# An encoder trunk in float32 on one core: ten by-k tiles, bias parts between pairs, and a wide form in layer 1

## The chip, the cores and the metric

The kernel runs on one core of a Trainium2 chip. The metric is the device time of one execution in microseconds (us); the profile is one execution taken by the hardware profiler. The core's engines are TensorE (PE in the profile; PEld is its weight load), VectorE (DVE), ScalarE (ACT), GpSimd (POOL) and SyncE (SP), which here issues all transfers from device memory.

## The reference

Two layers over 256 tokens of width 2048, all in float32. A conditioning vector gives six vectors of 2048 a layer, which shift, scale and gate.

```python
cond = jax.nn.silu(c)
for l in range(DEPTH):
    mod = cond @ w_ada[l] + b_ada[l]                 # 2048 x 12288
    sh_a, sc_a, g_a, sh_m, sc_m, g_m = split(mod, 6)
    h = _rmsnorm(x) * (1.0 + sc_a) + sh_a
    proj = h @ w_in[l]                               # dq, dk, dv, cq, ckv, kr
    ...                                              # two kinds of attention; one has a relative-position bias
    x = x + g_a * (concat(out_a, out_b) @ w_o[l])
    h = _rmsnorm(x) * (1.0 + sc_m) + sh_m
    x = x + g_m * (square(relu(h @ w_mlp_in[l])) @ w_mlp_out[l])
return _rmsnorm(x, final_norm_g)
```

## The kernel before

Activations lie as features by tokens: 16 slices (k) of 128 features by 256 tokens. A weight matrix is cut into tiles of 128 columns; a tile's product with all 16 slices is 16 products of 128x128 weights with 128x256 activations.

**Three forms of a product.** Float32 values are split into two fp32r parts, `hi` (ScalarE, L143, L575, L593) and `lo` (VectorE, L144, L581, L594). The *narrow* form (`mac`, L175 to 181) multiplies in three matmuls of 256 columns: hi by hi, hi by lo, lo by hi. The *wide* form (`wide`, L190 to 201) has hi and lo of the activations side by side: one matmul of 512 columns (L199) and one of 256 (L200), into a bank of its own whose two halves are added afterwards (`joined`, L864, or in the update itself). The *whole* form (L243) multiplies unsplit float32; the profile counts two matmuls for each of its products.

**By k.** After a norm the slices of h come one pair at a time, so the first product is done by k (`by_k`): for pair p (slices 2p, 2p+1) all open column tiles are multiplied and summed up in open PSUM banks (8 in all, tag `b`). Before the change this is 12 tiles in 6 banks, two to a bank, in both layers and for both norms: in layer 0's first norm in the whole form for pairs 0 to 5 (`WHOLE`) and narrow for pairs 6 and 7, elsewhere narrow. The remaining columns follow tile by tile; in the MLP in the wide form.

**The head.** `setup` broadcasts c, loads and transposes x, and prepares the position bias. The modulation vectors are sums on VectorE (L306): each 1 MB block of `w_ada` gives one slice of one vector, 192 blocks in all, loaded into the 5 `raw` buffers. `first_norm_then_by_k` (L630) needs for pair p four blocks: two for the shift (g 0), two for the scale (g 1); L316 finishes the scale. Then L573 makes the modulated pair `hf` on ScalarE. In the order of the program, pair p issues its weights (L224, in the `hi` and `lo` buffers, four of each), makes the marks of a bias part (L452, L456, L458), makes pair p+1 ready (L563, four blocks, L573, L575), multiplies (L243), and then has the work that `FILL` names for p: a bias part (L468, L469, 16 matmuls into bank `pb`, out by four copies L472), the lambdas or the rope tables. `EARLY` says after which pair the first three quarters of a second product (`w_d`, four tiles, `later`, two banks) are done in the whole form.

**Rates.** Later blocks of `w_ada` are loaded by credit: every call of `weights` adds `rate`, and each full credit issues one block, summed at the next call.

**Order.** Program order is the priority; the builder's scheduler may let a ready instruction pass one that it believes is waiting. `behind` adds an order by hand. Each engine then runs its queue in order; SyncE's queue too, so a transfer that waits for a buffer holds up all behind it.

Of the kernel before, what the change touches and what calls it, by code (L numbers as in the profile page):

```python
# [94 lines left out]
EARLY = {4: (0, 1), 6: (2,)}  # L95
# [3 lines left out]
RATE_A0, RATE_A1, RATE_A2, RATE_K, RATE_M = 1.1, 0.5, 0.7, 0.6, 0.66  # L99
FILL = "0|1|2|l3|r"  # L100


class Trunk:
# [142 lines left out]

    def tokens_by_k(self, pss, w, xs, first, last):
# [86 lines left out]
    def setup(self):  # L334
# [18 lines left out]
        for h in range(2):  # L353
            for t in range(2):
                xt[t][h] = self.wp.tile([P, D // 2], F32, tag=("hi", "lo")[h], name=self.name("xt"), bufs=4)
                nc.sync.dma_start(xt[t][h], io["x"][t, :, D // 2 * h : D // 2 * h + D // 2])
        self.bias_setup()
        self.rel = [self.bias_rel(0)]
        for j in range(4):
# [3 lines left out]
            nc.scalar.activation(self.cond[:, c], ps, AF.Silu)  # L363
        self.x = cp.tile([P, NK, T], F32, name="x")
        tot = self.sp.tile([P, 2, 2], F32, tag="s22", name="xsq")
# [4 lines left out]
        for h in range(2):  # L370
            for p in range(4):
# [6 lines left out]
                nc.scalar.activation(self.x[:, k : k + 2], ps, AF.Copy)  # L378
# [165 lines left out]
    def spread(self, out, r, tot, n):  # L544

        nc = self.nc
        nc.scalar.activation(r, tot, AF.Sqrt, bias=self.eps, scale=1.0 / n)
        nc.vector.reciprocal(r, r)
        for t in range(2):
# [3 lines left out]
            )  # L553

    def warm(self, a, n):
# [57 lines left out]
    def norm_then_by_k(self, l, acc, sh, sc, src, n):  # L613

        r = self.rstd(acc, D, True)
        banks = self.open_banks(2 * n)
        h = []
        for p in range(8):
# [6 lines left out]
            blocks = self.by_k_weights([src[l, p, b] for b in range(2)], 2 * n, False)  # L625
            self.by_k(banks, blocks, h, k, NK, 2 * n)
# [3 lines left out]
    def first_norm_then_by_k(self, acc, src, n, fill, early):  # L630
# [4 lines left out]
        self.spread(ps, s, s, D)  # L635
        self.nc.scalar.activation(r, ps, AF.Copy)
        banks = self.open_banks(2 * n)
# [14 lines left out]
        for p in range(8):  # L652
            blocks = self.by_k_weights([src[0, p, b] for b in range(2)], 2 * n, p < WHOLE)
# [7 lines left out]
            self.by_k(banks, blocks, h, 2 * p, NK, 2 * n, whole if p < WHOLE else None)  # L661
# [12 lines left out]
    def layer(self, l, acc):  # L674
# [86 lines left out]
        q += [self.copy(ps, "q", qs) for ps in banks[3:]]  # L761
# [52 lines left out]
        self.rate = RATE_K  # L814
        h, banks = self.norm_then_by_k(l, acc, 3, 4, io["w_m0"], 3)
# [48 lines left out]
    def joined(self, ps, out):  # L864
# [173 lines left out]
def _layout(i):  # L1038
# [20 lines left out]
    keep = {k: [] for k in ("w_a", "w_d", "w_t", "w_kr", "w_dv", "w_uq", "w_uk", "w_uv", "w_oa", "w_ob", "w_m0", "w_m1", "w_m2")}  # L1059
    for l in range(2):  # L1060
        w = f["w_in"][l]
        first = np.concatenate([w[:, 3072:3840], w[:, :768]], 1)
        keep["w_a"].append(np.stack([_kquarters(np.ascontiguousarray(first[:, 768 * j : 768 * j + 768]), 768, 2) for j in range(2)], 1))
# [14 lines left out]
        keep["w_m0"].append(np.stack([_kquarters(np.ascontiguousarray(w[:, 768 * j : 768 * j + 768]), 768, 2) for j in range(2)], 1))  # L1078
        keep["w_m1"].append(_ktiles(np.ascontiguousarray(w[:, 1536:])))
# [22 lines left out]
```

## Time and profile before

| | us |
|---|---|
| runs shown: median of 3 (lowest to highest) | 2238.89 (2238.78 to 2242.17) |
| the profiled execution, whole | 2236.08 |
| its span, first to last instruction | 2234.2 |
| TensorE busy | 2200.3 |
| VectorE busy | 1654.8 |
| ScalarE busy | 1131.5 |

In the views, a row gives engine, line, operation, tiles (out<-in), shapes and a count; in the timeline the first two numbers are start and length in us from the span's start, and what stands in brackets is the idle time ahead of it and what ended it. Matmuls are pipelined, so a row of one matmul is longer than the distance between two.

### The profile page before, as it was taken

To read this page: it belongs to the slowest core of one execution; us is meant where nothing else is said; L and a number is where in the kernel's file an instruction comes from. 1 tells how busy PE (TensorE), PEld (TensorE's weight loads), DVE (VectorE), ACT (ScalarE), POOL (GpSimd) and SP (SyncE) were. 2 spreads that over 40 slices of the span, in tenths; PEclk is the share of its full clock that TensorE was granted. 3 is DMA by queue.
4 is the path that set the end of the run, shared out by engine and by line. 5 is a ranking of instruction groups with operands and counts; after the bars stand their busy time and mean duration, and the time that the engine had idled before them with its cause. 6 is when DMAs were issued, how large, how long until landed. Compare 5 with 4: busy or idle time off the path is not lost.

```text
span 2234.2 us, 33164 instructions
## 1 busy us (share of the span) xinstructions
PE 2200.3 (98%) x13386; PEld 1963.3 (88%) x13386; DVE 1654.8 (74%) x2253; ACT 1131.5 (51%) x1681; POOL 1.9 (0%) x10
## 2 busy tenths in 40 slices
PE   7899999999999999999999999999999999999998
PEld 6799888998888888888899988989888888888887
DVE  7879779888878888887988776775665555565565
ACT  6545664465454355355445565544635534544553
POOL 0000000000000000000000000000000000000000
PEclk8999999999999999999999999999999999999998
DMA  9897778898887888888879666655555555555552
GB/s 387 330 379 286 282 282 316 307 352 318 315 313 300 321 306 316 319 313 309 308 265 350 250 241 226 238 201 202 191 189 191 188 186 186 189 188 189 190 187 76
DMA packets 85693, 585.55 MB, mean 262 GB/s; under 512 B 9505, under 2 KB 9889, under 8 KB 21409
## 3 DMA queue, kind: packets, MB, share of 16 engines
q1 hardware_dynamic: 85538, 583.42, 70.8%
q8 instruction: 105, 1.72, 0.3%
q14 instruction: 50, 0.41, 0.0%
HBM read 581.28 MB, written 2.10 MB: 261 GB/s over the span
## 4 chain that ended last, share of the span: by engine, by line
PE 93%; DVE 4%; ACT 2%; DMA 1%; issue 1%; SPq 0%; DVEq 0%; ACTq 0%
PE ps L199 41%; PE ps L200 21%; PE pk L180 4%; PE pk L181 4%; PE pk L179 4%; PE pk L243 3%; DVE ada L306 2%; PE pv L255 1%; PE pv L254 1%; PE pv L256 1%; DVE lo L144 1%; PE ps L179 1%; PE ps L180 1%; PE ps L181 1%; PE pw L559 1%; PE po L956 1%
## 5 line engine op out<-in xcount | busy, mean ns | idle before, releaser
L144 DVE TENSOR_TENSOR lo<-raw,hi 128x1024 fp32r<-128x1024 f32 (+1 forms) x722 | 853.7, 1185 | 434.4 <-ACT hi L143 428.4
L143 ACT ACTIVATE hi<-raw 128x1024 fp32r<-128x1024 f32 (+1 forms) x722 | 740.2, 1028 | 823.9 <-PE ps L199 612.6
L199 PE MATMUL ps<-hid,hi 128*128 128x512 f32 x2048 | 718.0, 395 | 0.0
L199 PE MATMUL ps<-h,hi 128*128 128x512 f32 x1664 | 581.5, 394 | 0.0
L200 PE MATMUL ps<-hid,lo 128*128 128x256 f32 x2048 | 574.1, 280 | 0.0
L200 PE MATMUL ps<-h,lo 128*128 128x256 f32 x1664 | 466.5, 280 | 0.0
L199 PEld LDWEIGHTS ps<-hid,hi 128*128 128x128 f32 x2048 | 383.9, 187 | 91.1 <-DVE hid L173 1.5
L306 DVE SCALAR_TENSOR_TENSOR ada<-ada,cond 128x2048 f32<-128x2048 f32 x192 | 438.1, 2284 | 3.7 <-DMA ada<-in_w_ada 3.7
L200 PEld LDWEIGHTS ps<-hid,lo 128*128 128x128 f32 x2048 | 387.0, 189 | 0.1
L199 PEld LDWEIGHTS ps<-h,hi 128*128 128x128 f32 x1664 | 311.8, 187 | 71.9
L200 PEld LDWEIGHTS ps<-h,lo 128*128 128x128 f32 x1664 | 314.4, 189 | 0.0
L180 PE MATMUL pk<-h,hi 128*128 128x256 f32 x704 | 199.0, 283 | 0.0
L181 PE MATMUL pk<-h,lo 128*128 128x256 f32 x704 | 198.9, 283 | 0.0
L179 PE MATMUL pk<-h,hi 128*128 128x256 f32 x704 | 198.6, 284 | 0.0
L862 DVE SCALAR_TENSOR_TENSOR x<-ps,mod,x 128x256 f32<-128x256 f32 x272 | 131.3, 483 | 64.0 <-PE ps L200 59.8
L180 PEld LDWEIGHTS pk<-h,hi 128*128 128x128 f32 x704 | 134.5, 191 | 0.1
L181 PEld LDWEIGHTS pk<-h,lo 128*128 128x128 f32 x704 | 134.5, 191 | 0.0
L179 PEld LDWEIGHTS pk<-h,hi 128*128 128x128 f32 x704 | 134.0, 191 | 0.1
L243 PE MATMUL pk<-hf,w 128*128 128x256 f32 x384 | 90.4, 399 | 12.8 <-ACT hf L573 12.8
L243 PEld LDWEIGHTS pk<-hf,w 128*128 128x128 f32 x384 | 76.9, 202 | 25.5 <-ACT hf L573 14.0
L199 PE MATMUL ps<-mo,hi 128*128 128x512 f32 x192 | 69.0, 398 | 0.0
L199 PE MATMUL ps<-do,hi 128*128 128x512 f32 x192 | 68.8, 398 | 0.0
(213 smaller groups left out, 2297.2 us busy)
## 6 DMA issues: line engine op xcount, KB each, us to landing
raw<-in_w_m SPq DMA_DIRECT2D x232, 1024.0 KB, 4.8
ada<-in_w_ada SPq DMA_DIRECT2D x192, 1024.0 KB, 5.0
raw<-in_w_ob SPq DMA_DIRECT2D x24, 1024.0 KB, 5.1
raw<-in_w_m SPq DMA_DIRECT2D x32, 768.0 KB, 5.8
raw<-in_w_dv SPq DMA_DIRECT2D x16, 1024.0 KB, 4.8
raw<-in_w_a SPq DMA_DIRECT2D x20, 768.0 KB, 6.1
raw<-in_w_t SPq DMA_DIRECT2D x12, 1024.0 KB, 5.2
w<-in_w_a SPq DMA_DIRECT2D x24, 384.0 KB, 12.3
```

Of the source, the lines that this page charges most:

```text
L143: nc.scalar.activation(hi, v, AF.Copy)
L144: ins = nc.vector.tensor_tensor(lo, v, hi.bitcast(F32), ALU.subtract)
L179: mm(ps, hi, x[0], start=first, stop=False, skip_group_check=shared)
L180: mm(ps, hi, x[1], start=False, stop=False, skip_group_check=shared)
L181: mm(ps, lo, x[0], start=False, stop=last, skip_group_check=shared)
L199: mm(ps.rearrange("p a b -> p (a b)"), hi, both, start=k == 0, stop=False)
L200: mm(ps[:, 0], lo, x, start=False, stop=k == nk - 1)
L243: self.nc.tensor.matmul(ps, v, whole[k], start=first, stop=last, skip_group_check=True)
L254: mm(ps, xh, hi, start=first and k == 0, stop=False)
L255: mm(ps, xh, lo, start=False, stop=False)
L306: ins = nc.vector.scalar_tensor_tensor(w, w, 1.0, self.cond, ALU.mult, ALU.mult, accum_out=acc[:, i : i + 1])
L862: self.nc.vector.scalar_tensor_tensor(x, ps[i][:, j], g[:, m + i : m + i + 1], x, ALU.mult, ALU.add)
```

## The change

Layer 0's first by-k product has 10 tiles in 5 banks instead of 12 in 6; the two tiles left out (`w_q0`) are done narrow, after the last quarter of `w_d`. The quarters of `w_d` move from pairs 4, 4 and 6 to pairs 1, 3 and 5, the bias parts from pairs 0, 1, 2, 3 to 0, 2, 4, 6, the lambdas to 5, the rope tables from 4 to 7. In `setup` one block of `w_ada` is loaded ahead of each half of x, ScalarE's table for the square root is loaded early, and the copies of x go behind the root. In layer 1 both by-k products are wide: six tiles in six banks, and six more tiles wide afterwards; no blocks of `w_ada` are loaded during them.

```diff
-EARLY = {4: (0, 1), 6: (2,)}
+EARLY = {1: (0,), 3: (1,), 5: (2,)}
...
-RATE_A0, RATE_A1, RATE_A2, RATE_K, RATE_M = 1.1, 0.5, 0.7, 0.6, 0.66
-FILL = "0|1|2|l3|r"
+RATE_A0, RATE_A1, RATE_A2, RATE_K, RATE_K1, RATE_M = 1.1, 0.5, 0.7, 0.6, 0.0, 0.66
+FILL = "0||1||2|l|3|r"
...
+    def wide_by_k(self, banks, blocks, xs, k0, nk):
+
+        mm = self.nc.tensor.matmul
+        n = len(banks)
+        (w, half), = blocks
+        for i in range(2 * half // (n * P)):
+            k = k0 + i
+            x, _, both = xs[k]
+            for j, ps in enumerate(banks):
+                c = (i * n + j) * P
+                hi, lo = (v[:, c % half : c % half + P] for v in w[c // half])
+                mm(ps.rearrange("p a b -> p (a b)"), hi, both, start=k == 0, stop=False)
+                mm(ps[:, 0], lo, x, start=False, stop=k == nk - 1)
...
         for h in range(2):
+            self.ada_load()
             for t in range(2):
...
+        self.warm(self.ones, 4)
...
+        nc.scalar.activation(self.s("root", 1), self.eps, AF.Sqrt)
+        self.ada_sums()
+        for _ in range(2):
+            self.ada_load()
...
-                nc.scalar.activation(self.x[:, k : k + 2], ps, AF.Copy)
+                self.turned.append(nc.scalar.activation(self.x[:, k : k + 2], ps, AF.Copy))
...
-            self.nc.tensor.matmul(ps, self.ident, a[:, :P], start=True, stop=True)
+            self.nc.tensor.matmul(ps, self.ones, a[:, :P], start=True, stop=True)
...
-            blocks = self.by_k_weights([src[l, p, b] for b in range(2)], 2 * n, False)
-            self.by_k(banks, blocks, h, k, NK, 2 * n)
+            blocks = self.by_k_weights([src[p, b] for b in range(2 - l)], 6, False)
+            if l == 0:
+                self.by_k(banks, blocks, h, k, NK, 6)
+            else:
+                self.wide_by_k(banks, blocks, h, k, NK)
...
-        self.spread(ps, s, s, D)
-        self.nc.scalar.activation(r, ps, AF.Copy)
-        banks = self.open_banks(2 * n)
+        root = self.spread(ps, s, s, D)
+        out = self.nc.scalar.activation(r, ps, AF.Copy)
+        for i, ins in enumerate(self.turned[1:]):
+            self.behind(ins, root if i < 2 else out)
+        banks = self.open_banks(n)
...
-            h, banks = self.first_norm_then_by_k(acc, io["w_a"], 3, fill, early)
+            h, banks = self.first_norm_then_by_k(acc, io["w_a"], 5, fill, early)
         else:
-            h, banks = self.norm_then_by_k(l, acc, 0, 1, io["w_a"], 3)
+            self.rate = RATE_K1
+            h, banks = self.norm_then_by_k(l, acc, 0, 1, io["w_a1"])
...
-        cqr = [self.copy(ps, "cqr") for ps in banks[:2]]
-        ckr = self.copy(banks[2], "ckr")
+        if l == 0:
+            cqr = [self.copy(ps, "cqr") for ps in banks[:2]]
+            ckr = self.copy(banks[2], "ckr")
+        else:
+            cqr = [self.joined(banks[i : i + 2], self.u("cqr")) for i in (0, 2)]
+            ckr = self.joined(banks[4:], self.u("ckr"))
...
-        q += [self.copy(ps, "q", qs) for ps in banks[3:]]
+        if l == 0:
+            q += [self.copy(ps, "q", qs) for ps in banks[3:]]
+            q.append(self.copy(self.pair([io["w_q0"][j] for j in range(2)], h), "q", qs))
+        else:
+            for i in range(0, 6, 2):
+                q.append(self.joined(self.wides([io["w_q1"][i + j] for j in range(2)], h), self.u("q"), qs))
...
-        self.rate = RATE_K
-        h, banks = self.norm_then_by_k(l, acc, 3, 4, io["w_m0"], 3)
+        self.rate = RATE_K1 if l else RATE_K
+        h, banks = self.norm_then_by_k(l, acc, 3, 4, io["w_m0"] if l == 0 else io["w_m01"])
...
+            done = 12 - 6 * l
-            for m in range(0 if fb else 12, NK, 2):
-                srcs = [io["w_m1"][l, NK * fb + m + j - 12] for j in range(2)]
+            for m in range(0 if fb else done, NK, 2):
+                srcs = [io[f"w_m1{l}"][NK * fb + m + j - done] for j in range(2)]
                 ps = self.wides(srcs, h)
+                if l:
+                    banks = [self.joined(banks[i : i + 2], self.t("sum")) for i in range(0, len(banks), 2)]
...
-            self.nc.scalar.activation(t, ps[i][:, 0], AF.Copy)
-            self.nc.vector.tensor_tensor(t, ps[i][:, 1], t, ALU.add)
+            self.nc.scalar.activation(t, ps[i][:, 0], AF.Copy, scale=scale)
+            self.nc.vector.scalar_tensor_tensor(t, ps[i][:, 1], scale, t, ALU.mult, ALU.add)
```

The layout of the weights in device memory follows (`w_a` for layer 0 in blocks of 640 columns, `w_a1`, `w_q0`, `w_q1`, `w_m01`, `w_m10`, `w_m11`).

More of the change, by code (lines that the diff above doesn't have):

```diff
@@ L553, in spread @@
             )
+        return ins
     def warm(self, a, n):
@@ L652, in first_norm_then_by_k @@
         for p in range(8):
-            blocks = self.by_k_weights([src[0, p, b] for b in range(2)], 2 * n, p < WHOLE)
+            blocks = self.by_k_weights([src[p, b] for b in range(2)], n, p < WHOLE)
             low = lows
@@ L1062, in _layout @@
         first = np.concatenate([w[:, 3072:3840], w[:, :768]], 1)
-        keep["w_a"].append(np.stack([_kquarters(np.ascontiguousarray(first[:, 768 * j : 768 * j + 768]), 768, 2) for j in range(2)], 1))
+        if l == 0:
+            a["w_a"] = np.stack([_kquarters(np.ascontiguousarray(first[:, 640 * j : 640 * j + 640]), 640, 2) for j in range(2)], 1)
+            a["w_q0"] = _ktiles(np.ascontiguousarray(first[:, 1280:]))
+        else:
+            a["w_a1"] = _kquarters(np.ascontiguousarray(first[:, :768]), 768, 2)[:, None]
+            a["w_q1"] = _ktiles(np.ascontiguousarray(first[:, 768:]))
         keep["w_t"].append(_ktiles(np.ascontiguousarray(w[:, 1280:2048])))
```

20 lines of the change are left out of this document (12 added, 8 removed).

## The prediction

> **What bounds the kernel now.** I began with the page's span and its chain of waits.
>
> ```profile
> span 2234.2 us, 33164 instructions
> ...
> PE 93%; DVE 4%; ACT 2%; DMA 1%; issue 1%; SPq 0%; DVEq 0%; ACTq 0%
> ```
>
> TensorE ends nearly every step; a gain is TensorE work saved or TensorE idling removed. The table by stretches then shows where it idles. Columns: length; busy time and instructions of PE, PEld, DVE, ACT, POOL; granted clock, DMA share, GB/s.
>
> ```profile
> 25.00:95.00 70.00, 61.48 (x258) 51.82 (x258) 55.52 (x89) 43.06 (x77) 0.53 (x1) 0.93 0.95 383
> ...
> 155.50:250.00 94.50, 91.61 (x689) 86.80 (x688) 85.98 (x155) 56.81 (x103) 0.00 (x0) 1.00 0.79 298
> 1151.00:1220.00 69.00, 69.00 (x577) 69.00 (x576) 61.96 (x83) 35.34 (x50) 0.00 (x0) 1.00 0.88 321
> 1502.00:1571.00 69.00, 69.00 (x577) 69.00 (x577) 41.54 (x61) 35.88 (x54) 0.00 (x0) 1.00 0.53 181
> 1570.00:1670.00 100.00, 100.00 (x578) 87.75 (x577) 62.79 (x82) 49.72 (x67) 0.00 (x0) 1.00 0.55 191
> ```
>
> It idles 8.5 us between 25 and 95, at a clock of 0.93, 2.9 in layer 0's attention, and not at all in layer 1's by-k products or MLP. So the head is read next: the timeline, TensorE alone.
>
> ```profile
> 25.47 13.52 PE L243 MATMUL pk<-hf,w 128*128 128x256 f32 x48 [4.61 <-ACT hf L573]
> 38.64 0.58 PE L468 MATMUL pb<-oh,lsch 128*128 128x512 f32 x1
> 42.51 10.52 PE L243 MATMUL pk<-hf,w 128*128 128x256 f32 x48
> 58.86 12.20 PE L243 MATMUL pk<-hf,w 128*128 128x256 f32 x48 [2.20 <-ACT hf L573]
> 77.60 10.63 PE L243 MATMUL pk<-hf,w 128*128 128x256 f32 x48 [2.75 <-ACT hf L573]
> 95.12 36.49 PE L243 MATMUL pk<-hf,w 128*128 128x256 f32 x160 [3.23 <-ACT hf L573]
> 140.08 7.07 PE L243 MATMUL pk<-hf,w 128*128 128x256 f32 x32
> 146.80 0.47 PE L179 MATMUL pk<-h,hi 128*128 128x256 f32 x1
> ```
>
> Each x48 is a pair, x160 is pair 4, two quarters of `w_d` and pair 5. TensorE waits for `hf` before pairs 0, 2, 3, 4 and never after 95.12, since the two quarters at pair 4 give it a backlog. What `hf` waits for is in VectorE's timeline.
>
> ```profile
> 39.80 0.16 DVE L316 SCALAR_TENSOR_TENSOR mod<-macc,vec 128x2 f32<-128x2 f32 x1
> ...
> 76.76 0.15 DVE L316 SCALAR_TENSOR_TENSOR mod<-macc,vec 128x2 f32<-128x2 f32 x1
> ...
> 94.28 0.15 DVE L316 SCALAR_TENSOR_TENSOR mod<-macc,vec 128x2 f32<-128x2 f32 x1
> ...
> 110.30 0.16 DVE L316 SCALAR_TENSOR_TENSOR mod<-macc,vec 128x2 f32<-128x2 f32 x1
> ...
> 122.82 0.16 DVE L316 SCALAR_TENSOR_TENSOR mod<-macc,vec 128x2 f32<-128x2 f32 x1
> ...
> 131.70 0.96 DVE L144 TENSOR_TENSOR lo<-raw,hi 128x768 fp32r<-128x768 f32 x1 [4.22 <-PE pk L243]
> ...
> 141.73 0.16 DVE L316 SCALAR_TENSOR_TENSOR mod<-macc,vec 128x2 f32<-128x2 f32 x1
> 143.36 0.76 DVE L581 TENSOR_TENSOR h<-hf,h 128x256 fp32r<-128x256 f32 x2 [1.47 <-ACT h L575]
> 144.40 3.80 DVE L144 TENSOR_TENSOR lo<-raw,hi 128x768 fp32r<-128x768 f32 x4 [0.28 <-ACT hi L143]
> ```
>
> L316 ends a pair's scale: 1, 3, 4, 5, 6 and 7. VectorE's modulation sums pace the head; a pair with a bias part takes 17.5 us (76.76 to 94.28), one without 12.5 (110.30 to 122.82).
>
> **Layer 1, wide for narrow.** In 1151 to 1220 TensorE runs narrow matmuls without a gap: 69 us over 576 steps is 0.1198, a product of three 0.359. In 1570 to 1670 wide ones: 100 over 577 is 0.1733, a product of two 0.347. Two by-k products of 12 tiles by 16 slices are 384 products at 0.0128: **-4.9**. No row shows wide matmuls in by-k order. They may cost 0.347, or as narrow ones 0.359, a gain between 4.9 and 0; I take the first, since shape and operands are those of the row. The Trainium skill, "TensorE: Matmul & The Clock Gate", section "Back-to-back issue gap", gives N/2.4 + 2.5 ns at full clock for an isolated matmul: 109 ns for 256 columns, 216 for 512, so 325 against 328 a product. By that the gain would be 1.0; the trace's 120 and 173 a matmul are above it and decide.
>
> What must keep up is VectorE. From its groups in the MLP's by-k stretch of layer 1:
>
> ```profile
> L144 DVE TENSOR_TENSOR lo<-raw,hi 128x768 fp32r<-128x768 f32 x28 | 26.8, 959 | 24.5 <-ACT hi L143 24.4
> L594 DVE SCALAR_TENSOR_TENSOR h<-ht,mod,h 128x256 fp32r<-128x256 f32 x15 | 6.7, 479 | 0.0
> L592 DVE SCALAR_TENSOR_TENSOR ht<-x,mod,pn 128x256 f32<-128x256 f32 x13 | 5.8, 474 | 0.0
> ```
>
> A wide pair is 12 products, 4.16 us of TensorE, and two of each of these, 3.82 of VectorE. It fits with 0.34 to spare, because no `w_ada` sums lie in it any more; were they there, as in 1151 to 1220 (VectorE 62 of 69), TensorE would wait. I charge 0.5, between 0 and the whole 4.9. **Layer 1: -4.4.** The sums that leave it and the joins (ScalarE and VectorE in place of a copy) land where VectorE has room:
>
> ```profile
> 1300.00:1400.00 100.00, 99.62 (x534) 84.92 (x534) 66.62 (x114) 59.95 (x119) 0.00 (x0) 1.00 0.65 233
> ```
>
> Nothing for these, then; without that cover the sums alone, 16 calls at a rate of 0.66, would be 10.6 x 2.29, 24 us of VectorE.
>
> **The start.** One block of `w_ada` goes ahead of each half of x, so first sums come earlier and x later. But all four blocks and x are needed for pair 0, and their bytes are the same.
>
> ```profile
> 4.38 3.11 SPq L290 DMA_DIRECT2D ada<-in_w_ada  x4
> ...
> DMA to landing us min/median/max: 7.9/13.3/15.0
> ```
>
> The fourth block, issued by 7, lands near 22; its sum and `hf` lead to 25.47 then as now. The root's table load and the matmuls of ones lie beside that transfer. 0, between -1 and +1 (x, late by two blocks, could become the last).
>
> **The head.** VectorE's groups, 25 to 142:
>
> ```profile
> L306 DVE SCALAR_TENSOR_TENSOR ada<-ada,cond 128x2048 f32<-128x2048 f32 x28 | 63.7, 2286 | 1.2 <-DMA ada<-in_w_ada 1.2
> L458 DVE TENSOR_SCALAR oh<-sq,K 128x512 fp32r<-128x512 f32 x16 | 7.7, 486 | 9.4 <-ACT sq L452 8.9
> ...
> L438 DVE SCALAR_TENSOR_TENSOR rel<-fl,rt 128x256 f32<-128x256 f32 x6 | 2.6, 478 | 0.0
> ...
> L437 DVE TENSOR_SCALAR rt<-fh 128x256 f32<-128x256 f32 x6 | 1.9, 348 | 0.0
> L441 DVE TENSOR_SCALAR rel<-rel 128x512 f32<-128x512 f32 x3 | 1.3, 420 | 0.0
> ```
>
> A bias part adds marks (4 x 0.486) and positions (2 x 0.478, 2 x 0.348, 0.42): 4.0. On 12.5 minus its small waits that is 15.3 of work, and 17.5 is seen: VectorE waits for ScalarE's squares, which queue behind three copies of the part before. In the new order a pair without a part lies between, and those copies are done. A marked pair thus takes 15.3 to 17.5; I take 16.0. An unmarked pair could be held by transfers:
>
> ```profile
> DMA packets 2757, 14.85 MB, mean 424 GB/s; under 512 B 303, under 2 KB 303, under 8 KB 1330
> ```
>
> That is 25 to 60, full. Four blocks and ten tiles are 4.19 + 1.31 MB, 13.0 us at that rate; with a quarter of `w_d` (1.05 MB) 15.4, which falls into marked pairs. So 12.9 unmarked, 16.0 marked. Pair 1 ends at 39.80 less the 2.1 of positions, which move back: 37.7. Pairs 2, 4, 6 are unmarked, 3, 5, 7 marked: 37.7 + 38.7 + 48.0 = **124.4** for pair 7's scale, now 141.73. Then 3.6 to the first split weights (141.73 to the first of the four at 144.40) and 20 narrow products, 7.2: the by-k product ends at 135.2. TensorE alone would need from 25.5: six pairs of 8.8 (ten twelfths of 10.52), three quarters of 7.1, four bias parts of 3.9 (38.64 to 42.51), 14.4 narrow, 3.0 of slow clock at pair 0 (13.52 against 10.52): 107, ending 132.5. So VectorE still sets the end. Now it ends at 146.80 + 24 x 0.36 = 155.4, but with two more tiles, which cost 32 x 0.359 = 11.5 later: 135.2 + 11.5 = 146.7. **-8.7** (-10.8 at 15.3, -4.2 at 17.5).
>
> **What comes after.** The rope tables, 17 small operations, lie today where TensorE has its backlog; these are the first and the last, and a half of that later quarter's split, with its pause.
>
> ```profile
> 94.08 0.29 DVE L483 CAST ang<-pos 128x256 f32<-128x256 int32 x1
> ...
> 103.16 0.29 DVE L499 TENSOR_SCALAR cc<-cc 128x256 f32<-128x256 f32 x1
> ...
> 152.47 1.22 DVE L144 TENSOR_TENSOR lo<-raw,hi 128x1024 fp32r<-128x1024 f32 x1 [0.94 <-ACT hi L143]
> ```
>
> At 0.3 to 0.4 they are 5.5 us, and behind pair 7 only the last quarter of `w_d` and `w_q0` cover them. In front of that quarter's split they would cost 5.5, in its pauses nothing. Two more calls of `weights` at 1.1 draw 2.2 sums forward, 5 us, into 155 to 250, where VectorE has 8.5 free of 94.5 and TensorE already idles: 0 to 5. **+3** for both, below the middle: four halves with 0.94 each and the 1.47 at 143.36 give the tables 5 us of pauses.
>
> **The sum.** -4.4 - 8.7 + 3.0 = -10.1 on 2234.2 is 2224.1. The execution itself took 1.9 more than its span, 2236.1, and the runs shown have their median 2.8 above that: **2229**.
>
> **Rivals.**
>
> A, the gain of the head is lost. A marked pair stays at 17.5, as three rows of today, and the rope tables and sums are paid at 6: -4.4 - 4.2 + 6 = -2.6, 2236. For it: ScalarE's order in the queue is not mine to see. Against: the copies do leave the pair.
>
> B, slower: `w_d`'s quarters hold weight buffers. They take one `hi` and one `lo` of four between two pairs, and the next pair's weights wait for TensorE with four blocks of `w_ada` behind them on SyncE. The wait exists: 4.22 on VectorE at 131.70, and on SyncE (in all, times, longest)
>
> ```profile
> SPq L224 <- PE pk L243: 12.3, 4, 5.6
> ```
>
> At 5 each, three times, pair 7's scale comes at 139.4 and the time is 2244. It is slower from 134.5 on. Against: TensorE, with two tiles less a slice, reaches each release 10 us or so before VectorE needs the block.
>
> C, the change is not what it says in layer 1: in by-k order wide products take as long as narrow ones, or wait for the split slices, and the 4.4 are lost: 2233.
>
> **How the numbers follow.** Forecast 0.6, A 0.2, C 0.12, B 0.08. A measurement tells 0.2%, 4.5 us, from no change: faster is under 2234.4, slower over 2243.4. Forecast and nearly all of C are faster, 0.72; A and the mild part of B are the same, 0.21; the rest slower, 0.07. The forecast's own ends are 2223 (marked pairs at 15.3, nothing for rope tables, sums and layer 1's 0.5) and 2234 (marked pairs at 17.5); with A the range is 2222 to 2238.
>
> **What would show it.** Right: L316 of pair 7 at 122 to 129, TensorE's waits for `hf` under 8 us between 25 and 135, wide by-k stretches at 0.173 a matmul without idle, end of the head's by-k product near 135. Wrong in the head: L316 of pair 7 past 134, marked pairs still 17.5, or waits of L224 on SyncE longer than 12. Wrong in layer 1: idle before L144 or L594 with TensorE waiting for `h`. Wrong behind it: idle in layer 0's attention well above 2.9.

## The result, and the profile after

The changed kernel takes 2247.32 us (median of 6; 2242.0 to 2250.52) against 2238.84 (median of 6; 2236.4 to 2242.17): 1.0034 of the time before, 95% interval 1.002 to 1.0049. The forecast was 2229, its range 2222 to 2238. The profiled execution took 2248.31, with a span of 2246.5.

TensorE still ends nearly every step, as the page's span and chain of waits show; VectorE's share of the chain has grown from 4% to 6%.

```profile
span 2246.5 us, 32477 instructions
...
PE 90%; DVE 6%; ACT 2%; DMA 1%; issue 0%; SPq 0%; DVEq 0%; ACTq 0%
```

The same stretches as before the change (columns as there; the by-k stretches of layer 1 lie some 12 us later):

```profile
25.00:95.00 70.00, 65.91 (x292) 56.72 (x293) 56.21 (x80) 32.79 (x60) 0.00 (x0) 0.97 1.02 422
155.50:250.00 94.50, 87.22 (x640) 82.47 (x639) 83.61 (x151) 51.31 (x94) 0.00 (x0) 0.98 0.81 300
1163.00:1232.00 69.00, 69.00 (x457) 63.38 (x458) 51.41 (x73) 34.84 (x49) 0.00 (x0) 1.00 0.67 240
1513.00:1582.00 69.00, 68.96 (x390) 59.81 (x391) 54.29 (x84) 44.49 (x74) 0.00 (x0) 1.00 0.68 240
1582.00:1682.00 100.00, 100.00 (x568) 86.59 (x567) 59.60 (x73) 43.86 (x53) 0.00 (x0) 1.00 0.52 183
```

TensorE idles less at the head's beginning (4.1 us in place of 8.5), but 7.3 in place of 2.9 from 155.5 to 250. Layer 1's by-k products run wide and without a gap, as meant. But a wide matmul takes 100/568 = 0.176 us in the last row, where the prediction had read 0.173 at the same place before: the wide form itself, which the change leaves alone, has become slower in this execution.

TensorE's rows of the head, and the last scale's place in VectorE's:

```profile
25.52 10.77 PE L243 MATMUL pk<-hf,w 128*128 128x256 f32 x40 [5.83 <-ACT hf L595]
41.29 24.44 PE L243 MATMUL pk<-hf,w 128*128 128x256 f32 x112 [1.35 <-ACT hf L595]
71.62 24.44 PE L243 MATMUL pk<-hf,w 128*128 128x256 f32 x112 [2.21 <-ACT hf L595]
101.42 8.90 PE L243 MATMUL pk<-hf,w 128*128 128x256 f32 x40 [1.71 <-ACT hf L595]
...
110.30 7.15 PE L243 MATMUL pk<-hf,w 128*128 128x256 f32 x32
```

```profile
133.06 0.16 DVE L330 SCALAR_TENSOR_TENSOR mod<-macc,vec 128x2 f32<-128x2 f32 x1
```

L330 is the old L316, the end of a pair's scale. Pair 7's comes at 133.06, 8.7 earlier than before (141.73), but 8.7 later than forecast (124.4). Where the time goes is read from one marked pair, pair 3, in VectorE's timeline (L320 is a modulation sum, L479 a mark, L473 on ScalarE a square):

```profile
51.90 0.16 DVE L330 SCALAR_TENSOR_TENSOR mod<-macc,vec 128x2 f32<-128x2 f32 x1
51.98 0.87 DVE L459 SCALAR_TENSOR_TENSOR rel<-fl,rt 128x256 f32<-128x256 f32 x2
...
54.20 0.42 DVE L603 TENSOR_TENSOR h<-hf,h 128x256 fp32r<-128x256 f32 x1
57.52 1.10 DVE L479 TENSOR_SCALAR oh<-sq,K 128x512 fp32r<-128x512 f32 x2 [2.90 <-ACT sq L473]
58.54 2.28 DVE L320 SCALAR_TENSOR_TENSOR ada<-ada,cond 128x2048 f32<-128x2048 f32 x1
...
70.77 0.16 DVE L330 SCALAR_TENSOR_TENSOR mod<-macc,vec 128x2 f32<-128x2 f32 x1
```

18.9 us, with 2.90 of idling while ScalarE makes squares. Before the change the squares started later behind the scale, but a sum lay under that wait, as VectorE's timeline of before shows for the pair from 76.76 on:

```profile
79.38 2.29 DVE L306 SCALAR_TENSOR_TENSOR ada<-ada,cond 128x2048 f32<-128x2048 f32 x1
...
83.69 1.10 DVE L458 TENSOR_SCALAR oh<-sq,K 128x512 fp32r<-128x512 f32 x2 [2.01 <-ACT sq L452]
```

In the new order all four sums of pairs 3 and 5 stand behind their first two marks. Pair 7, the third marked pair (114.67 to 133.06), is made up otherwise: VectorE's waits there are 1.1 us in all and a sum does stand in front, but the weights of pair 6's narrow products are split in it (L144, four times), 3.2 us.

```profile
117.83 1.55 DVE L144 TENSOR_TENSOR lo<-raw,hi 128x640 fp32r<-128x640 f32 x2
119.95 0.82 DVE L144 TENSOR_TENSOR lo<-raw,hi 128x640 fp32r<-128x640 f32 x1 [0.56 <-ACT hi L143]
120.69 2.29 DVE L320 SCALAR_TENSOR_TENSOR ada<-ada,cond 128x2048 f32<-128x2048 f32 x1
...
122.90 0.82 DVE L144 TENSOR_TENSOR lo<-raw,hi 128x640 fp32r<-128x640 f32 x1
123.64 0.88 DVE L479 TENSOR_SCALAR oh<-sq,K 128x512 fp32r<-128x512 f32 x2
```

### The profile page after: what moved, and what is told of

The parts are those of the page before. It is cut to its first block, busy times and chain, and to the rows that moved or that the text cites. A ratio compares the mean times of both kernels' runs of the same rounds, so it can differ in the third digit from the quotient of the medians.

```text
span 2246.5 us, 32477 instructions
## 1 busy us (share of the span) xinstructions
PE 2208.5 (98%) x13034; PEld 1944.1 (87%) x13034; DVE 1665.9 (74%) x2273; ACT 1138.5 (51%) x1697; POOL 1.9 (0%) x10
## 4 chain that ended last, share of the span: by engine, by line
PE 90%; DVE 6%; ACT 2%; DMA 1%; issue 0%; SPq 0%; DVEq 0%; ACTq 0%
PE ps L199 44%; PE ps L200 22%; DVE ada L320 3%; PE pk L179 2%; PE pk L180 2%; PE pk L181 2%; PE pk L258 2%; PE pv L268 1%; PE pv L269 1%; PE pv L270 1%; DVE lo L144 1%; PE pk L259 1%; ACT sq L473 1%; PE ps L179 1%; PE ps L180 1%; PE ps L181 1%
## 5 line engine op out<-in xcount | busy, mean ns | idle before, releaser
L144 DVE TENSOR_TENSOR lo<-raw,hi 128x1024 fp32r<-128x1024 f32 (+2 forms) x718 | 855.6, 1195 | 428.5 <-ACT hi L143 426.5
L143 ACT ACTIVATE hi<-raw 128x1024 fp32r<-128x1024 f32 (+2 forms) x718 | 740.4, 1035 | 816.0 <-PE ps L199 615.6
L199 PE MATMUL ps<-h,hi 128*128 128x512 f32 x1856 | 654.6, 398 | 0.0
L200 PE MATMUL ps<-h,lo 128*128 128x256 f32 x1856 | 520.4, 280 | 0.1
L320 DVE SCALAR_TENSOR_TENSOR ada<-ada,cond 128x2048 f32<-128x2048 f32 x192 | 437.7, 2283 | 1.6 <-ACT cond L379 1.6
L199 PEld LDWEIGHTS ps<-h,hi 128*128 128x128 f32 x1856 | 348.7, 188 | 86.1
L200 PEld LDWEIGHTS ps<-h,lo 128*128 128x128 f32 x1856 | 350.3, 189 | 0.5 <-DVE lo L144 0.5
L179 PE MATMUL pk<-h,hi 128*128 128x256 f32 x312 | 88.4, 287 | 5.2 <-ACT h L597 5.2
L181 PE MATMUL pk<-h,lo 128*128 128x256 f32 x312 | 88.9, 285 | 1.0 <-DVE lo L144 1.0
L180 PE MATMUL pk<-h,hi 128*128 128x256 f32 x312 | 89.0, 286 | 0.0
L243 PE MATMUL pk<-hf,w 128*128 128x256 f32 x336 | 75.7, 387 | 11.1 <-ACT hf L595 11.1
L915 ACT ACTIVATE relu<-sum 128x512 f32<-128x512 f32 x58 | 36.7, 632 | 72.1 <-DVE sum L910 72.1
L258 PE MATMUL pk<-h,hi 128*128 128x512 f32 x192 | 67.4, 396 | 0.1
L181 PE MATMUL ps<-h,lo 128*128 128x256 f32 x224 | 64.5, 288 | 0.8 <-DVE lo L144 0.8
```

Source lines behind the costliest of these rows:

```text
L143: nc.scalar.activation(hi, v, AF.Copy)
L144: ins = nc.vector.tensor_tensor(lo, v, hi.bitcast(F32), ALU.subtract)
L179: mm(ps, hi, x[0], start=first, stop=False, skip_group_check=shared)
L180: mm(ps, hi, x[1], start=False, stop=False, skip_group_check=shared)
L181: mm(ps, lo, x[0], start=False, stop=last, skip_group_check=shared)
L199: mm(ps.rearrange("p a b -> p (a b)"), hi, both, start=k == 0, stop=False)
```

## The experiments

Eighteen runs. Those with one execution are read from their profiles; "kr" is the start of the first kr product (end of the head), "psc" and "pom" the first score product and the first product of a head's output, "norm" the first warm matmul (a product into bank `pw` that nothing reads) of layer 0's MLP norm.

**Each kernel once more.** No edit.

> The changed kernel as it is, profiled once more. Theory P: a wide product in the MLP takes 0.3467 or 0.3533 us over a whole stretch, and which of the two is drawn anew where TensorE waits for hid, whatever the kernel; then the eight stretches (four in each layer, from one start of hid products to the next) are not all the same as in the first profile, where seven were slow, and the span moves by about 3.4 us for each. Rival Q: the pace belongs to the changed program; then seven or eight of eight are slow again. Both: the first MLP norm's warm matmuls start at 423, within 1.5.

> The kernel before as it is, profiled once more. Theory P: the number of slow stretches, four of eight in its first profile, changes, or other stretches are slow; the span moves by about 3.4 us for each. Rival Q: the same four are slow. Both: the first MLP norm's warm matmuls start at 417.5, within 1.5.

Measured: 2243.07 and 2235.66. The starts of successive wide products show two paces, 346.7 and 353.3 ns, each constant over whole stretches and redrawn at the waits for `hid` between `w_m1` and `w_m2`. They fell differently than in the first profiles of the same kernels, most of all in the changed one. The norm starts at 422.2 and 414.2, 8.0 us apart where the first profiles had 5.4 (422.9 and 417.5): the changed kernel's came as expected, that of before 3.3 earlier than expected.

**One part of the change at a time.** The other part is undone, the rest stays.

```diff
 # e3: layer 1 alone
-EARLY = {1: (0,), 3: (1,), 5: (2,)}
-FILL = "0||1||2|l|3|r"
+EARLY = {4: (0, 1), 6: (2,)}
+FILL = "0|1|2|l3|r"
...
 # e4: layer 0 alone
-    blocks = self.by_k_weights([src[p, b] for b in range(2 - l)], 6, False)
+    blocks = self.by_k_weights([src[p, b] for b in range(2)], 6, False)
...
```

> Layer 1's wide by-k products and their rates alone; layer 0 and the start as before. Theory S (layer 0's part costs 5.4, layer 1's gains): the warm matmuls of the first MLP norm start at 417.5 as before; layer 1's attention stage is 1 to 2.5 us shorter than 351.4; time 2233 to 2238 against 2239. Rival R (wide form in by-k order waits for the split slices): idle of TensorE in the two stretches, time over 2240.

> Layer 0's part and the start alone; layer 1's products narrow as before. Theory S: the warm matmuls of the first MLP norm start at 423, and the time is 4 to 7 us over the kernel before, 2243 to 2246, apart from the pace in the MLPs. Rival: the loss by then is an accident of one profile; time 2239, within 2.

Measured: layer 1 alone 0.9974 (0.9949 to 1.0), layer 0 alone 1.0023 (1.0005 to 1.0042). The norm starts at 414.5 and 424.1. So layer 0's part is what costs, by 8 to 10 us before the first MLP begins. The times themselves missed: medians of 2225.76 and 2238.56 against 2233 to 2238 and 2243 to 2246, and the second by itself would speak for the rival; layer 1's attention was 0.5 us shorter (350.9), not 1 to 2.5. But single times of one kernel lay 19 us apart (2222.6 to 2241.79 for e3), too far for the size of either part.

**The head: positions.** First the positions of the next part were put into the unmarked pair (e5; e6 with the rope tables in pair 5 as well), then all four parts' into the setup (e9).

```diff
-FILL = "0||1||2|l|3|r"
+FILL = "0|a|1|b|2|lc|3|r"        # e5: a, b, c make the positions of parts 1, 2, 3
+FILL = "0|a|1|b|2|lcr|3|"        # e6
...
-        self.rel = [self.bias_rel(0)]
+        self.rel = [self.bias_rel(a) for a in range(4)]   # e9
```

> The changed kernel with one thing moved: the relative positions of the next bias part (L459, L462) are made in the pair without a part (pairs 1, 3, 5) and no longer in the pair that marks it. Theory H: the marked pairs of the head take 18.3 to 18.9 us because ScalarE's squares wait for positions that VectorE makes only after the scale of the next pair; then they fall to 16 us or less, the unmarked ones grow by at most 2 us, pair 7's scale comes at 124 to 128 us in place of 133.1, and the first kr product at 156 to 160 in place of 162.9 to 163.3. Rival K (the bias copies in ScalarE's queue, or the weights' landing, set the marked pairs): they stay at 18 to 19 us, pair 7's scale stays at 131 to 134. The whole time by itself tells little (one execution, 2235 to 2247).

> As the run before, and the rope tables made in pair 5 and not in pair 7. Theory V (from 142 to 260 us VectorE sets the pace of layer 0's attention, so all that is added to its queue there delays TensorE by as much): VectorE's busy time from 142 to 163 us falls by about 3 us, and the first product of the output of the heads (pom, 257.7 to 258.4 in the changed kernel) comes 2 to 4 us earlier than in the run before. Rival W (weights' landing sets it): pom comes at the same distance after the first kr product as in the run before, 94 to 96 us.

> The changed kernel with all four parts' relative positions made in the setup, where VectorE idles 9 of the first 25 us; so no L459 or L462 stands behind a scale in the head. Moving them between pairs (run e5) had left them at the very place in VectorE's order where they were, so that run decided nothing. Theory H (squares wait for positions, VectorE for squares): marked pairs 14 to 16 us in place of 18.3 to 18.9, pair 7's scale (L330) at 121 to 127 in place of 133.1, first kr product 2 us or more earlier than 163. Theory D (the head's transfers set its pace: 36.2 MB between the scales of pairs 1 and 7 at 390 GB/s are 92.8 us, and 92.6 were seen): marked pairs shrink a little and unmarked ones grow, so that the scales of pairs 1 and 7 stay 89 to 93 us apart.

Measured. e5: kr 163.3, pair 7's scale 133.3, the positions' rows still right behind the scale (52.46 behind 52.38): the edit left the instructions in the order they had, so it tells nothing of theory H. e6: kr 165.9, pom 262.0; the rope tables cost 2.6 us in pair 5, in front of TensorE, and give nothing back behind the head: pom comes 96.1 after kr (94.9 in e5), at rival W's 94 to 96 and against theory V's forecast. e9 did move the positions: VectorE goes from the scale straight to `h` and the marks.

```profile
54.25 0.16 DVE L330 SCALAR_TENSOR_TENSOR mod<-macc,vec 128x2 f32<-128x2 f32 x1
55.88 0.76 DVE L603 TENSOR_TENSOR h<-hf,h 128x256 fp32r<-128x256 f32 x2 [1.46 <-ACT h L597]
56.55 0.88 DVE L479 TENSOR_SCALAR oh<-sq,K 128x512 fp32r<-128x512 f32 x2
...
60.47 1.10 DVE L479 TENSOR_SCALAR oh<-sq,K 128x512 fp32r<-128x512 f32 x2 [2.31 <-ACT sq L473]
...
71.24 0.16 DVE L330 SCALAR_TENSOR_TENSOR mod<-macc,vec 128x2 f32<-128x2 f32 x1
```

That marked pair takes 17.0, not 14 to 16, and VectorE waits 2.31 for the squares even so; pair 5 takes 17.0 too, and pair 7 takes 19.5, longer than in the changed kernel. Theory H is refuted as to the positions; they are worth 1.9 and 1.4 us of pairs 3 and 5, and putting them at the start makes pair 0 late by 2.9 (28.4), so nothing is gained: pair 7's scale at 133.3, kr 164.5. Pairs 1 to 7 span 90.5 us in place of 92.6, inside theory D's bounds.

**The head: transfers.** Two quarters of `w_d` go behind the head.

```diff
-EARLY = {1: (0,), 3: (1,), 5: (2,)}
+EARLY = {1: (0,)}
```

> The changed kernel with the second and third quarter of w_d loaded and multiplied behind the head (EARLY holds quarter 0 alone): 2.1 MB less lie before pair 7's scale, one quarter in each of the marked pairs 4 and 6. Theory D (transfers set the marked pairs): these two take 15.5 to 16.5 us in place of 18.3 and 18.4, and pair 7's scale comes at 127 to 129.5. Theory H (the chain scale, positions, squares, marks on VectorE and ScalarE sets them): they stay at 18 to 18.5, pair 7's scale stays at 132 to 134. Either way the quarters cost later, as split products: the whole is no gain.

Measured: pair 5's scale comes 16.1 after pair 4's (18.4 in the changed kernel), pair 6's 15.8 (14.1), pair 7's 18.5 (18.4), and pair 7's scale at 132.5; kr 175.6, whole 2256.26. One marked pair answers to the transfers as D says, the last does not, and the lambdas' wait in pair 6 (4.1 in place of 2.4) eats most of the gain. My naming of the pairs in the expectation was off by one: the marked pairs are 3, 5 and 7. Pair 3, whose quarter stayed, takes 18.9 as before. What the missing quarter did for pair 5 stands in the rows. In the changed kernel SyncE issues the quarter, then four loads of `w_a`, which take 6.8 us, 5.1 of them waiting for weight buffers that TensorE still reads, then pair 5's four blocks. In e11 the same four loads take 2.2 and the blocks go 6.1 earlier (the changed kernel first):

```profile
68.46 1.22 SPq L224 DMA_DIRECT2D w<-in_w_d  x2
69.79 6.77 SPq L224 DMA_DIRECT2D w<-in_w_a  x4
76.65 3.69 SPq L304 DMA_DIRECT2D ada<-in_w_ada  x4
```

```profile
68.22 2.16 SPq L224 DMA_DIRECT2D w<-in_w_a  x4
70.53 9.57 SPq L304 DMA_DIRECT2D ada<-in_w_ada  x4
```

And in e11 a sum stands in front of pair 5's first marks again, so that VectorE waits 0.69 for the squares and not 2.90:

```profile
84.63 2.29 DVE L320 SCALAR_TENSOR_TENSOR ada<-ada,cond 128x2048 f32<-128x2048 f32 x1
...
87.62 1.10 DVE L479 TENSOR_SCALAR oh<-sq,K 128x512 fp32r<-128x512 f32 x2 [0.69 <-ACT sq L473]
```

So neither theory alone: the quarter sets pair 5, by way of SyncE's queue and the order of VectorE's, and pair 7 keeps its length.

**Layer 0's attention: VectorE.** In e7 the rate of modulation blocks is lower up to the values and higher behind; in e10 the weights of `w_q0` draw none.

```diff
 # e7 (1.1 throughout before); 1.35 from the values on
-RATE_A0 = 1.1
+RATE_A0, RATE_V0 = 0.7, 1.35
...
 # e10
+            self.rate = 0.0
             q.append(self.copy(self.pair([io["w_q0"][j] for j in range(2)], h), "q", qs))
+            self.rate = RATE_A0
```

> The changed kernel with the rate of modulation blocks in layer 0's attention at 0.7 a weight up to the values and 1.35 behind it, in place of 1.1 throughout: about 6 blocks of 2.2 us move behind 250 us. Theory V: VectorE has about 13 us less to do from 163 to 250, the distance from the first score product (psc, 176) to the first pom falls from 82 us to 74 to 78, and the first warm products of the MLP's norm come at 415 to 419 in place of 422.2 to 422.9. Rival W: the distance stays at 80 to 83 us, and the norm stays at 421 to 424.

> The changed kernel, but the two weights of w_q0 draw no modulation blocks (rate 0 while they are loaded), so that VectorE has 2.2 sums less, 5 us, between 145 and 260. Theory V (VectorE sets the pace of layer 0's attention): first score product (psc) to first pom 76 to 79 us in place of 82, first warm products of the MLP's norm at 417 to 420 in place of 422.2 to 422.9. Rival X (the sums are paid later all the same, as in run e7): pom earlier by 3 or more, but the norm's warm products at 421 or later.

The distance from psc to pom as a window, for the changed kernel, for before, for e7 and for e10:

```profile
176.40:258.40 82.00, 75.99 (x542) 71.32 (x542) 73.17 (x137) 47.78 (x92) 0.00 (x0) 0.98 0.81 300
```

```profile
175.00:252.50 77.50, 74.61 (x542) 69.65 (x542) 71.28 (x135) 47.63 (x91) 0.00 (x0) 1.00 0.83 310
```

```profile
176.80:252.10 75.30, 74.88 (x542) 69.97 (x542) 62.28 (x125) 46.52 (x91) 0.00 (x0) 1.00 0.69 257
...
325.00:430.00 105.00, 96.47 (x561) 84.47 (x560) 93.90 (x118) 40.19 (x59) 0.00 (x0) 0.95 0.85 316
```

```profile
181.00:257.00 76.00, 74.27 (x545) 70.02 (x544) 70.58 (x136) 47.36 (x91) 0.00 (x0) 1.00 0.83 315
```

The same 542 matmuls (545 with the edges of e10's window): the fewer sums VectorE has there, the less TensorE idles (6.0, 2.9, 0.4, 1.7). Theory V holds for this stretch, and the two calls of `w_q0` account for the whole loss in it. But e7 pays its sums at 325 to 430, where VectorE then is busy 93.9 of 105 us and TensorE idles 8.5: norm at 430.0, whole 2252.36, so its forecast of 415 to 419 failed. In e10 psc to pom is 75.7, but the norm comes at 420.9 (422.2 and 422.9 in the changed kernel), between V's 417 to 420 and rival X's 421 or later; part of the gain went in a slow clock ahead of psc (last section).

**The pace of the wide products.** e8 takes the layer 1 part alone and puts the last three of 16 steps of the first two `w_m2` products behind the first 13 of both; e13 is the same once more, e12 has other rates besides (0.95, then 1.2).

```diff
-        return [self.wide(src, xs) for src in srcs]
+        for ks in (range(nk - 3), range(nk - 3, nk)):      # first pair of each w_m2 block
+            for ps, w in zip(pss, ws):
+                for k in ks: ...                           # hi by both, lo by x, as in wide
```

> The kernel with the layer 1 part alone, and in the first pair of products of every w_m2 block the last three of 16 steps of both products put behind the first 13 of both, so that TensorE no longer waits for the last hidden tiles. Theory P (the pace of a wide pair, 346.7 or 353.3 ns, is drawn anew wherever TensorE waits, and otherwise stays): the pace of a whole MLP is then one and the same from its first w_m1 products to its end, the 0.1 us waits at the eight boundaries are gone, and since the pace behind the norm has been the long one in every run, both MLPs come out at the long pace: 728 to 732 us each, and the whole 2232 to 2242, slower than the layer 1 part alone (2225.8). Theory Q (the pace belongs to the stretch's addresses or to its place in the program): the w_m2 stretches go on changing between the two paces as before, and the whole is at or up to 2 us below 2225.8.

> The kernel of run e8 once more, profiled anew. Theory P (one pace for each whole MLP, drawn where TensorE last waited ahead of it): in the profile each MLP again has one pace throughout, long or short, not necessarily the same as in e8 (layer 0 long, layer 1 short), and the single times fall into groups 13 to 14 us apart (four stretches of 512 products at 6.6 ns), most of them near 2229 as before. Theory Q (bound to the place in the program): layer 0 long and layer 1 short in the profile again, and no groups.

> The kernel of run e8 (layer 1 part alone, no wait in w_m2), with the rate of modulation blocks in layer 0's attention at 0.95 up to the values and 1.2 behind them in place of 1.1: about 2 blocks move from the stretch before 250 us to that behind it. Theory V (VectorE is the bound in both stretches): the distance from psc to pom falls from 77.6 to 74 to 76 us, and the attention output behind it loses nothing to 3 us, so the first warm products of the norm come at 411 to 416 (e8: 414.3). Rival: as in run e7 more is lost behind than is gained in front, the norm at 417 or later. With the pace of the MLPs as in e8 the whole is 2224 to 2232.

Measured. A window in layer 0's MLP and one in layer 1's, e8 and then e13:

```profile
700.00:800.00 100.00, 100.00 (x568) 86.67 (x567) 83.31 (x99) 38.93 (x39) 0.00 (x0) 1.00 0.81 299
1700.00:1800.00 100.00, 100.00 (x579) 88.19 (x578) 57.95 (x75) 54.41 (x79) 0.00 (x0) 1.00 0.54 190
```

```profile
700.00:800.00 100.00, 100.00 (x568) 86.67 (x567) 83.71 (x99) 39.80 (x41) 0.00 (x0) 1.00 0.80 298
1700.00:1800.00 100.00, 100.00 (x568) 86.77 (x567) 57.35 (x74) 55.02 (x81) 0.00 (x0) 1.00 0.54 189
```

TensorE is busy throughout at full clock in all four, with 568 or 579 matmuls in the same 100 us. Within an MLP the pace no longer changes: in e8 every stretch of layer 1 went at 346.7, in e13 every one at 353.3. The times fall into two groups: e8 nine of 10 at 2226.8 to 2231.6 and one at 2243.1, e13 two at 2228.5 and 2229.5 and ten at 2241.6 to 2245.5, e12 five at 2231.5 to 2232.7 and seven at 2244.7 to 2249.0. Theory P holds and Q falls, though P's forecast of the long pace for both MLPs in e8 was half wrong. The ratios to before (0.9949, 0.9933 to 0.9965; 1.0014, 0.9999 to 1.003; 1.0008, 0.9988 to 1.0027) only tell which group was hit more often. In e12 psc to pom stayed at 77.7, against V's 74 to 76, and its norm at 417.7 (e8 414.3, e13 413.4), where the rival had it, shows no gain from the rates.

**Another order of the matmuls.** On top of e8, wide products go two by two: hi of k and k+1, then lo of both (e14); and eight by eight (e15).

```diff
-        for k in range(nk): hi(k); lo(k)
+        for k0 in range(0, nk, 2):
+            hi(k0); hi(k0 + 1)
+            lo(k0); lo(k0 + 1)
```

> The kernel of run e8 with the wide products ordered two by two: two matmuls of 512 columns, then the two of 256 that belong to them, in place of turns of 512 and 256. Columns and weight loads are the same in number. Theory A (the two paces come of the turns of a long and a short matmul against something with a period of its own): the pace changes, to one value or to other ones, anywhere from 340 to 360 ns a product. Theory B (it is the TensorE's own rate in that execution, whatever the order): 346.7 or 353.3 again, the times in two groups 13 to 14 us apart.

> The same with groups of eight: eight matmuls of 512 columns, then eight of 256 (in the first pair of each w_m2 block groups of 8, 5 and 3). Theory A: a long run of one shape goes at that shape's own pace, so the product costs one value in all executions, 340 to 360 ns, and the times no longer fall into two groups. Theory B: 346.7 or 353.3 and two groups, as before.

Measured: 2219.8 (2218.8 to 2220.33), 0.9917 (0.9903 to 0.9932); and 2224.81 (2223.46 to 2225.82), 0.9942 (0.9925 to 0.9958). The two groups are gone, and the pace is one and the same in both MLPs (e14):

```profile
700.00:800.00 100.00, 100.00 (x576) 87.24 (x575) 86.09 (x104) 41.45 (x44) 0.00 (x0) 1.00 0.85 318
1700.00:1800.00 100.00, 100.00 (x576) 87.25 (x574) 57.76 (x74) 51.72 (x71) 0.00 (x0) 1.00 0.54 190
```

Theory A holds: the order of long and short matmuls makes the two paces. e14's 347 ns is near the short pace, so its pace alone would not tell; e15 has 573 and 574 matmuls in these windows, 349 ns, and no second group came in the four executions of each or in the 17 below.

**The change with the pace held still.** The two edits of e14 on the kernel of before, on the changed kernel, and on the layer 1 part alone, on one chip.

> The kernel of before with its wide products by twos and without the wait in w_m2 (as in run e14), so that their pace has one value and no longer covers what the change does; neither part of the change is in it. Theory S (the layer 0 part costs 7 to 9 us, of which head 3 and attention 4 to 5, and the layer 1 part gains 1 to 3): 1 to 3 us above run e18, single times within 3 us of each other. Rival: the layer 1 part gains the 4.4 us that were predicted, and this run is 4 to 5 us above e18.

> The changed kernel with the same two edits; both parts of the change are in it. Theory S: 7 to 9 us above e18 (layer 0's part alone) and 5 to 8 above e16 (the whole change). Rival R (the loss of 8.5 us was drawn paces above all): within 3 us of e16.

> The kernel of run e14 again, the layer 1 part of the change alone: 2218 to 2222, and the fastest of the three by 1 us or more under theory S.

| | e16 before | e17 after | e18 layer 1 alone |
|---|---|---|---|
| median, us | 2224.34 | 2230.82 | 2220.14 |
| lowest to highest | 2223.66 to 2228.37 | 2229.01 to 2232.32 | 2219.74 to 2221.83 |
| runs | 6 | 6 | 5 |
| profiled: pair 7's scale | 141.9 | 133.0 | 137.9 |
| profiled: kr | 162.4 | 163.9 | 158.3 |
| profiled: psc to pom | 77.5 | 81.8 | 77.5 |
| profiled: norm | 416.5 | 423.5 | 412.4 |
| profiled: norm to end of span | 1810.0 | 1806.2 | 1805.5 |

The layer 1 part gains 4.2, the layer 0 part costs 10.7, the whole change 6.5; rival R falls. In the profiles e17's norm comes 11.1 behind e18's: 5.6 of it are there at kr, 1.8 come between kr and psc (14.7 against 12.9, at a granted clock of 0.88 against 1.00), 4.2 from psc to pom, and 0.5 go back behind it. Theory S was right on layer 0 within 2 us and wrong on layer 1: the rival's 4.4 was true. e16's profile is its slowest execution, with a head 4 us longer than in e18, whose head is the same program; kr was at 162.2 in the first profile of before and at 159.8 in its second.

e18 and e14 are the fastest versions here, 0.991 (0.9895 to 0.9925) and 0.9917 of the kernel before; in e18's run that kernel's median was 2241.04.

## Why the prediction was wrong

**Layer 1: right.** Forecast -4.4, measured -4.2 with the pace held still. Without that it could not be seen. The by-k stretch of layer 1's MLP, narrow in e16 and wide in e18:

```profile
1500.00:1565.00 65.00, 65.00 (x544) 65.00 (x543) 37.73 (x53) 32.95 (x48) 0.00 (x0) 1.00 0.56 191
```

```profile
1495.00:1560.00 65.00, 65.00 (x376) 56.78 (x375) 55.32 (x85) 43.53 (x73) 0.00 (x0) 1.00 0.75 268
```

0.1195 and 0.1729 a matmul, the prediction's 0.1198 and 0.1733. TensorE does not wait for VectorE there. Rival C is out. But the 0.173 was read in a stretch that had drawn the short pace; at the long one a wide product gains 6 ns and not 13. In the changed kernel's first profile only one of eight w_m2 stretches had the short pace, in that of before four; at 3.4 us each (512 products by 6.6 ns) that is 10 us between those two profiles that are not the change's. Of the 8.5 us between the medians of the result, 6.5 remain with the pace held still.

**The start: right.** 25.47 before, 25.52 after.

**The head: this step failed.** Forecast -8.7; kr went from 162.2 to 163.3 in the first profiles, from 158.3 to 163.9 in e18 and e17; it lies at 158.1 to 162.4 in the nine profiles that have the head and the rates of before and at 162.9 to 163.9 in the four that have the changed ones. The term mis-sized is the marked pair: "16.0", between 15.3 and 17.5; it is 18.9, 18.4 and 18.4, which is 7.7 of the 8.7 us by which pair 7's scale missed 124.4. The upper end was too low by the profile of before itself: 17.5 is the shortest of its three pairs that mark a part and make positions, and the two ahead of it, 39.80 to 76.76, take 18.5 on average. Pair 1's scale came at 40.44, not 37.7: of the 2.1 us of positions taken off, only 0.7 (L437) stood ahead of 39.80, and they still stand ahead of the scale (L458). The unmarked pairs (11.5, 11.5, 14.1) gave back 1.6 against 12.9 each.

The reason stated, that squares queue behind bias copies, was half of it. The copies do leave, and the squares begin 2.4 us after the scale (51.90 to 54.32) instead of 3.7 (76.76 to 80.48), as ScalarE's timeline of before and then of after shows (L472 a bias copy, L452 and L473 squares):

```profile
78.67 1.78 ACT L472 ACTIVATE bias<-pb 32x512 f32<-32x512 f32 x3
80.48 1.34 ACT L452 ACTIVATE sq<-rel,K 128x512 f32<-128x512 f32 x2
```

```profile
53.09 0.71 ACT L597 ACTIVATE h<-hf 128x256 fp32r<-128x256 f32 x2
54.32 1.33 ACT L473 ACTIVATE sq<-rel,K 128x512 f32<-128x512 f32 x2 [0.53 <-DVE rel L462]
```

But they still stand behind the scaled slice on ScalarE, and the sum that had covered VectorE's wait went behind the marks. Taking a delay out of the queue that is waited for gains nothing if the cover goes as well. That is the step that failed in pairs 3 and 5. The prediction counted the bytes of a quarter of `w_d` ("15.4, which falls into marked pairs") and not what it does to SyncE's queue, ahead of the pair's blocks. In e11, without that quarter, the sum stood in front again and pair 5 took 16.1, the forecast's 16.0. Pair 3 was not tried in this way, and no run kept a quarter and put the sum in front. In pair 7 the prediction put the split of the narrow weights at nothing; it is 3.2 us of VectorE.

TensorE left room for the forecast. In e18's head it is idle 8.4 us and in e17's 10.1:

```profile
25.50:158.30 132.80, 124.39 (x650) 110.51 (x650) 107.20 (x157) 69.06 (x118) 0.53 (x1) 0.98 0.95 380
```

```profile
25.50:163.90 138.40, 128.31 (x674) 113.74 (x675) 114.47 (x165) 71.02 (x121) 0.53 (x1) 0.94 0.94 374
```

Two tiles done narrow in place of whole are 1.9 us less for TensorE: 32 products at 0.359 come, 48 whole matmuls at 0.219 (two to a product) and 8 narrow products go, and the counts agree (96 more, 48 and 24 fewer, 674 against 650). That it is busy 3.9 longer all the same goes with the granted clock, 0.94 against 0.98: 6% of 138.4 us and 2% of 132.8 differ by 5.6, about the 3.9 + 1.9 to be explained. So at one clock this change could gain up to 8.4 + 1.9 = 10.3 in the head, near the 11 of the prediction's "TensorE alone" figure; that bound did not bind. VectorE did: pair 7's scale came 8.7 earlier in the first profiles and 4.9 earlier in e17 than in e18, where 17.3 were forecast, and from it to kr, where the two tiles now lie, it takes 9.8 and 10.5 longer (8.6 were forecast). The first profile of before also had one of the latest heads, with kr 2 to 4 us behind seven of the eight others that have it; why these differ was not tried.

**Behind the head: right in kind, too small.** Forecast +3 for rope tables and blocks. From psc to pom 4.5 were lost in the first profiles and 4.2 in e17. Of the 4.5, 3.1 are idling (6.0 against 2.9) and 1.4 a slower TensorE for the same 542 matmuls at clock 0.98. e10 lays it on the blocks that `w_q0`'s weights draw; e6 shows that the rope tables were no cheaper in pair 5.

**The rivals.** B was on the right side. Its wait exists: SyncE's queue, 25 to 142, after (in all, times, longest):

```profile
SPq L224 <- PE pk L243: 19.6, 8, 3.4
```

12.3 before. The transfers were at a share of 1.02 from 25 to 95 meanwhile, so the wait left no gap in them there. But B named the mechanism that e11 shows in pair 5: with the quarter, the next loads of `w_a` wait for buffers and the blocks behind them go out late. It cost 2.2 there, through the order of VectorE's queue, and not B's 5. A foresaw the head's loss of half its gain, not of all.

## What to carry to other kernels

Before pricing a new order, take TensorE's idle time in that stretch, less the work that the new order adds: at one granted clock no gain can exceed it. It is a bound and not a forecast; here it was 10.3, and the engine that TensorE waits for kept all of it. So price that engine's queue, waits and all, pair by pair, from every row there is. When a delay ahead of a waiting instruction is removed, look for the work that lay under the wait and where it will stand afterwards. And when single times of one program differ by more than the effect, find what varies and hold it still: here two edits in the order of matmuls brought the spread of a kernel from 19 us (e3) to 2 (e18) and made a difference of 4 us plain.

## What the runs showed of the hardware

A wide product (a matmul of 512 columns, one of 256) in turns settles on 346.7 or 353.3 ns at full granted clock, keeps it for hundreds of us, and changes only where TensorE waits, if only for 0.1 us; not every such wait changes it. Where successive starts were read they repeat every three products, 347, 347, 346 or 349, 350, 361 ns (e8, e13); the changed kernel's one short stretch has 350, 343. Taking the waits out froze the pace of a whole MLP; two matmuls of 512 followed by two of 256 had one pace, about 347 ns by 576 matmuls in 100 us. Why there are two was not found. The Trainium skill, "TensorE: Matmul & The Clock Gate", section "Back-to-back issue gap", gives a single gap for each number of columns, and says that in a kernel it is set by the matmul together with its weight load; both paces here lie above the 325 ns that its formula for an isolated matmul gives, and the runs do not show a single value.

The granted clock fell in some executions after a short wait and not in others. In e10 TensorE waited 2.03 us up to 164.3, and the next stretch went at 0.80; in e7 it waited as long up to 163.1, and the clock stayed at 1.00 (kr to psc, e10 and then e7):

```profile
165.50:181.00 15.50, 15.50 (x109) 15.50 (x109) 10.21 (x17) 6.47 (x11) 0.00 (x0) 0.80 0.40 144
```

```profile
164.00:176.80 12.80, 12.80 (x110) 12.80 (x109) 9.04 (x14) 6.82 (x11) 0.00 (x0) 1.00 0.31 99
```

The same products took 15.5 and 12.8 us. What decides was not tried.
